# Order of the out-projection's units, and the tiles of two weight sums, in a short-convolution layer

## The chip, the cores and the metric

One core of a Trainium2 chip runs the whole program. The metric is the device time of one execution in microseconds (us): the median of three runs, 1556.54 us before the change (1554.22 to 1557.58).

## What is computed

With these sizes `DEPTH` is 1, so only layer 0 and the final norm run:

```
x: 1024 tokens x 2048
h = rmsnorm(x, norm0_w)
b, c, u, z = split(h @ w_in, 4)             # w_in 2048 x 8192
conv = causal depthwise width-3 convolution of (c * u)
y = b * conv * silu(z)
x = x + y @ w_out                           # w_out 2048 x 2048
out = rmsnorm(x, norm_f_w)
```

## The kernel before

Both projections are done with fewer products than the plain scheme needs. Operands are cut in two along each axis, and seven products of sums of the quarters take the place of eight. Every float32 operand is split in a high part (a copy made by ScalarE, line 111) and a low part (a subtraction on VectorE, line 112), and a product takes three passes: high by high, high by low, low by high.

The program is a list of *steps*, here called units. A unit loads weights (and operands), makes sums, splits, issues 24 matmuls of 512 columns and evacuates the sums from PSUM. The loop of lines 796 to 822 walks over the list: at unit i it issues the loads of some units ahead (line 798), the splits up to unit i + 2, the matmuls and the evacuation of unit i, one *chore* (`chore_at`) and up to two pieces of `background` work. The framework then orders each engine's instructions by readiness, and it places the waits. Tiles come from pools: `t4` (16 tiles of 4 KB a partition, for loads, sums and the 2 `wf` tiles), `xp` (14 of 8 KB, of which the 8 row blocks `st` hold one each at the end) and `wp` (3 of 8 KB, split weights). A tile is given again when its last reader is done, a storing DMA included.

*The chores.* During the in-projection's first half the chores form sums of `w_out` and store them in DRAM: `out_weights` loads the four quarters `wp` (line 706), forms four sums (lines 714 to 719) and stores each (`td`, line 711, issued by GpSimd). All of it runs on VectorE between the splits of the in-projection. The tile named `b[0, 0]` takes the first, the third and the fourth sum, one over the other.

*The out-projection.* It has 32 units of a first kind (`out_step`: four u for each of eight pairs r, db) and then 21 of a second kind (`out_second`: product p of z). Units of the first kind compute four of the seven products of the outer cut: r, in halves db, accumulated over u in four PSUM banks. They load 1 MB (two transfers, pieces of 4 and 2 KB) and split two tiles. The units of the second kind do the other three outer products z, each again by seven (p). They load 1.5 MB (three transfers, pieces of 1 and 2 KB), split three tiles, and end each with two adds of a bank to `st`. A group of the first kind ends at u = 3 with 4 or 8 adds to `st` (line 545). When a block of `st` is complete it is squared for the norm (line 548) and multiplied by the norm's weight (`weigh`, line 555). The last block of a row block calls `finish` (line 739): the scale by the row's norm and two output stores, one from SP's queue and one from ScalarE's. SP's queue also issues all loads, in order.

*Order.* Before, all 32 units of the first kind run ahead of the 21 of the second, and the groups of the first kind take turns on banks `po` 0 to 3 and 4 to 7 (line 579). Units of the second kind use pairs of banks by a table (line 647).

Of the kernel before, what the change touches and what calls it, by code (L numbers as in the profile page):

```python
# [10 lines left out]
AF = mybir.ActivationFunctionType  # L11
ALU = mybir.AluOpType
# [5 lines left out]
NB = 512  # L18
# [23 lines left out]
def hybrid_kernel(  # L42
# [48 lines left out]
    def f4(name, dtype=F32):  # L91
        return t4.tile([P, 1024], dtype, name=name, tag="t4")
# [445 lines left out]
    yv = y_dram.rearrange("(u j h) p t -> h p u j t", j=2, h=2)  # L538
    sv = s_dram.rearrange("u j p s t -> u p j s t")

    def result(th, tb, chunk, ps, final, now, last, scratch):

        cols = slice(chunk * NB, (chunk + 1) * NB)
        v = st[th, tb][:, cols]
        add(v, ps, v)
        if not final:
            return
        nc.scalar.activation(scratch if scratch is not None else ps, v, AF.Square, accum_out=sums[th, tb][:, chunk:chunk + 1])
        if last:
            finish(th, tb, chunk)  # L550
            return

        def weigh():
            c = chunk % 2 * NB
            nc.vector.tensor_tensor(v, v, wf[chunk // 2][:, c:c + NB], op=ALU.mult)

        if now:
            weigh()
        else:
            scaled.append(weigh)  # L560

    def out_step(r, db, u):

        w = {}

        def loads():
            w["b"] = f4(f"wo_{db}_{r}_{u}")
            nc.sync.dma_start(w["b"], w_out[db, 0, 0, u] if r == 1 else t_dram[r][db, u])
            w["y"] = f4(f"ys_{db}_{r}_{u}")
            src = yv[0, :, u, :, ycols[0]] if r == 1 else sv[u, :, :, S_SLOT[r]]  # L570
            nc.sync.dma_start(w["y"].rearrange("p (j t) -> p j t", j=2), src)

        def split_w():
            w["w"] = hl(wp, f"wo_{db}_{r}_{u}")
            split(w["b"], w["w"][:, 0, :], w["w"][:, 1, :])
            w["yh"] = hl(xp, f"Y_{db}_{r}_{u}")
            split(w["y"], w["yh"][:, 0, :], w["yh"][:, 1, :])

        first = 4 * (db if r != 5 else 1 - db)

        def mm():
            open_banks()
            for jj in range(2):
                for tb in range(4):
                    for yz, wz in PASSES:
                        nc.tensor.matmul(  # L586
                            po[first + tb],
                            w["yh"][:, yz, jj * NB + tb * P:jj * NB + (tb + 1) * P],
                            w["w"][:, wz, jj * NB:(jj + 1) * NB],
                            start=(r in (1, 5) and u == 0 and jj == 0 and yz == 0 and wz == 0),  # L590
                            stop=(r in (7, 5) and u == 3 and jj == 1 and yz == 1),
                            skip_group_check=True,
                        )

        def evac():
            if u < 3:
                return
            dest = {1: [(0, 0)], 5: [(0, 1), (1, 1)], 6: [(0, 1)], 7: [(1, 0), (1, 1)]}[r]
            sq = f4(f"sq_{db}")[:, 0:NB] if r == 7 else None
            for tb in range(4):  # L600
                for th, dh in dest:
                    result(th, tb, 2 * dh + db, po[first + tb], r == 7 and dh == 1, False, False, sq)

        return Step(loads, nothing, split_w, mm, evac)

    def out_second(z, p):
# [37 lines left out]
                split(w["b"][v], t[:, 0, :], t[:, 1, :])  # L644
                w["w"].append(t)

        pair = {2: (0, 1, 2), 3: (3, 2, 1), 4: (0, 1, 2)}[z]["acb".index({5: "c", 3: "c", 2: "b"}.get(p, "a"))]
        end = z == 4 and p == 4

        def mm():  # L650
# [10 lines left out]
                    )  # L661

        def evac():
            t2, db, final = {
                1: (0, 0, False), 5: (1, 1, False), 6: (0, 1, False), 2: (0, 0, True),
                7: (1, 1, True), 3: (0, 1, True), 4: (1, 0, True),
            }[p]
            sq = f4(f"sqz_{z}")[:, 0:NB] if p == 7 else None
# [29 lines left out]
    def out_weights(db, u):  # L698
# [9 lines left out]
        def diff(r, o, x0, x1):  # L708
# [86 lines left out]

    for i, s in enumerate(steps):
        early = i < 2
        upto("load", i + (2 if i < 4 else 3 if i < 8 else LOAD_AHEAD + 1 if i < first_out - 8 else 5))
        while late:
            reload_x(late.pop(0))  # L800
        if i == 8 + 7 * 15 - 1:
            reload_x(PRODUCTS[-1])
        n = i - first_out
        for db in range(2):
            m = n - 9 * db
            if m in (-1, 0, 4, 5):
                for tb in range(2):
                    open_rows(int(m > 0), tb + 2 * (m in (0, 5)), db)
# [52 lines left out]
```

## Time and profile before

| | |
|---|---|
| three timed runs | 1554.22, 1556.54, 1557.58 us |
| the profiled execution's own time | 1551.41 us |
| its span, first to last instruction | 1549.6 us |
| granted TensorE clock, mean | 0.995 of full speed |
| PE busy, VectorE busy, ScalarE busy | 98%, 74%, 35% |
| out-projection's matmuls in the trace | 1246.14 to 1536.85 us |

TensorE is busy nearly all the time, so its busy share says little. What can be read is how many matmuls start in a stretch: at full pace 111 or 112 in 25 us, since 24 matmuls take 5.44 us. A stretch with fewer has a wait in it or a lower granted clock. In the rows, `PEld` is TensorE's weight load and `SPq`, `POOLq`, `ACTq` are DMA issues of these engines' queues. A helper records splits (line 112), sums (115) and adds (118), so tiles tell which work a row is.

### The profile page before, as it was taken

The numbers are of one execution on the slowest core, as the hardware profiler recorded it, in microseconds if no ns is written. First come the engines' busy times: TensorE is split into PE (matmuls) and PEld (weight loads), VectorE is DVE, ScalarE is ACT, GpSimd is POOL, SyncE is SP. The second block draws the span as 40 slices with busy tenths as digits, with TensorE's granted clock in tenths as the row PEclk, the third lists the DMA queues.
The fourth block names the chain that finished last, engine by engine and source line by source line (L and its number), as shares of the span: only waits on it lengthen the run. The fifth ranks groups of instructions, "written<-read, shape, count | busy, mean of one in ns | idle before, by whom it ended". The sixth has DMA issues, their size and how long they took to land.

```text
span 1549.6 us, 17709 instructions
## 1 busy us (share of the span) xinstructions
PE 1525.7 (98%) x6705; PEld 1259.1 (81%) x6705; DVE 1141.2 (74%) x1321; ACT 542.0 (35%) x660; POOL 128.2 (8%) x234
## 2 busy tenths in 40 slices
PE   9999999999899999999999999999999999999996
PEld 7878888888688888888888888888888888888884
DVE  6798676776666565457878788887888786568996
ACT  5544343332233333322222222222222334344674
POOL 0001111111111110110000000000000120000000
PEclk9999999999999999999999999999999999999998
DMA  9606677998877665794436444643454679665875
GB/s 364 247 28 212 240 266 271 368 352 329 289 279 257 218 232 176 282 410 150 134 129 201 152 128 138 202 151 114 161 179 163 247 255 396 221 208 189 278 238 228
DMA packets 114277, 351.95 MB, mean 227 GB/s; under 512 B 11008, under 2 KB 22288, under 8 KB 112400
## 3 DMA queue, kind: packets, MB, share of 16 engines
q1 hardware_dynamic: 81040, 223.38, 43.0%
q0 software_dynamic: 31712, 122.72, 20.5%
q10 hardware_dynamic: 1440, 4.73, 0.8%
q8 instruction: 52, 0.85, 0.2%
q14 instruction: 33, 0.27, 0.1%
HBM read 243.83 MB, written 106.96 MB: 226 GB/s over the span
## 4 chain that ended last, share of the span: by engine, by line
PE 71%; issue 14%; DMA 5%; DVE 5%; POOL 3%; ACT 0%; SPq 0%; POOLq 0%; DVEq 0%; ACTq 0%
PE pa L481 32%; PE pc L481 16%; PE po L586 11%; PE pb L481 8%; PE po L654 4%; DMA xsq<-in_x_dram 2%; DMA xr<-in_x_t_dram 1%; POOL td L711 1%; POOL xd L179 1%; POOL pd L513 1%; DMA out_dram<-st 1%; DVE X L112 1%; DMA wz<-w 1%; DVE xc L348 0%; DVE wzh L112 0%
## 5 line engine op out<-in xcount | busy, mean ns | idle before, releaser
L481 PE MATMUL pa<-X,w 128*128 128x512 f32 x2880 | 670.3, 390 | 6.8 <-DVE g L118 5.7
L481 PEld LDWEIGHTS pa<-X,w 128*128 128x128 f32 x2880 | 542.0, 188 | 120.5 <-issue 6.1
L481 PE MATMUL pc<-X,w 128*128 128x512 f32 x1440 | 336.4, 389 | 0.0
L481 PEld LDWEIGHTS pc<-X,w 128*128 128x128 f32 x1440 | 270.3, 188 | 56.1
L112 DVE TENSOR_TENSOR w<-wi,w 128x1024 fp32r<-128x1024 f32 x150 | 183.1, 1222 | 116.1 <-ACT w L111 115.3
L111 ACT CAST w<-wi 128x1024 fp32r<-128x1024 f32 x150 | 157.0, 1049 | 230.8 <-PE pa L481 131.3
L586 PE MATMUL po<-wo,Y 128*128 128x512 f32 x768 | 174.2, 389 | 0.0
L586 PEld LDWEIGHTS po<-wo,Y 128*128 128x128 f32 x768 | 144.2, 188 | 29.9
L481 PE MATMUL pb<-X,w 128*128 128x512 f32 x720 | 168.3, 389 | 0.0
L481 PEld LDWEIGHTS pb<-X,w 128*128 128x128 f32 x720 | 135.1, 188 | 28.4 <-DVE w L112 0.4
L111 ACT CAST w<-wt 128x1024 fp32r<-128x1024 f32 x60 | 63.3, 1055 | 242.1 <-PE pb L481 108.2
L118 DVE TENSOR_TENSOR g<-pa,g 128x512 f32<-128x512 f32 x150 | 102.5, 686 | 28.3 <-PE pa L481 27.3
L654 PE MATMUL po<-wzh,Yz 128*128 128x512 f32 x504 | 114.7, 389 | 2.1 <-DVE st L118 2.1
L654 PEld LDWEIGHTS po<-wzh,Yz 128*128 128x128 f32 x504 | 94.5, 188 | 22.1 <-issue 2.5
L507 ACT COPY g<-pa 128x512 f32<-128x512 f32 x90 | 53.0, 588 | 139.0 <-PE pa L481 138.7
L115 DVE TENSOR_TENSOR wt<-wi,wi 128x1024 f32<-128x1024 f32 x60 | 73.4, 1223 | 34.3 <-DMA s_dram<-g 15.2
L368 PE MATMUL pc<-xc,wc 128*128 128x512 f32 x384 | 87.5, 390 | 1.1 <-DVE wc L353 1.1
L368 PEld LDWEIGHTS pc<-xc,wc 128*128 128x128 f32 x384 | 71.9, 188 | 17.2 <-issue 2.0
L112 DVE TENSOR_TENSOR w<-wt,w 128x1024 fp32r<-128x1024 f32 x60 | 73.2, 1220 | 10.0 <-ACT w L111 10.0
L118 DVE TENSOR_TENSOR g<-pc,g 128x512 f32<-128x512 f32 x90 | 61.5, 686 | 22.4 <-PE pc L481 22.4
L115 DVE TENSOR_TENSOR wp<-wp,wp 128x1024 f32<-128x1024 f32 x32 | 38.9, 1221 | 46.0 <-issue 28.2
L112 DVE TENSOR_TENSOR wo<-wo,wo 128x1024 fp32r<-128x1024 f32 x32 | 39.1, 1222 | 35.8 <-ACT wo L111 35.8
(110 smaller groups left out, 1058.3 us busy)
## 6 DMA issues: line engine op xcount, KB each, us to landing
wi<-in_w_in_dram SPq DMA_DIRECT2D x120, 512.0 KB, 5.0
pd<-g POOLq DMA_DIRECT2D x60, 512.0 KB, 5.6
g<-pd SPq DMA_DIRECT2D x60, 512.0 KB, 4.7
wp<-in_w_out_dram SPq DMA_DIRECT2D x32, 512.0 KB, 6.7
td<-wp POOLq DMA_DIRECT2D x32, 512.0 KB, 5.7
xd<-xo POOLq DMA_DIRECT2D x28, 512.0 KB, 5.9
X<-xd POOLq DMA_DIRECT2D x14, 1024.0 KB, 10.8
w<-wq POOLq DMA_DIRECT2D x24, 512.0 KB, 4.0
```

The lines of the kernel that those rows point to most:

```text
L111: nc.scalar.copy(h, raw)
L112: nc.vector.tensor_tensor(l, raw, h.bitcast(F32), op=ALU.subtract)
L115: nc.vector.tensor_tensor(o, a, b, op=ALU.subtract)
L118: nc.vector.tensor_tensor(o, a, b, op=ALU.add)
L179: nc.gpsimd.dma_start(x_dram[r][:, j], o)
L368: nc.tensor.matmul(state["ps"][2 * s + gi][h], wv[:, wz, gi, jj, s, :], xs[:, xz, h * NB:(h + 1) * NB], start=(a == 0 and jj == 0 and wz = ...
L481: nc.tensor.matmul(ps[where, s], wv[:, wz, j, s, :], xt[:, j % 2, xz, :], start=(r in (1, 5, 2) and j == 0 and wz == 0 and xz == 0), stop= ...
L507: nc.scalar.copy(o, ps[where, s])
L513: nc.gpsimd.dma_start(p_dram[c][i], g[i])
L586: nc.tensor.matmul(po[first + tb], w["yh"][:, yz, jj * NB + tb * P:jj * NB + (tb + 1) * P], w["w"][:, wz, jj * NB:(jj + 1) * NB], start=(r ...
L654: nc.tensor.matmul(po[2 * pair + tb], w["yh"][:, yz, u * 256 + tb * P:u * 256 + (tb + 1) * P], w["w"][u // 2][:, wz, (u % 2) * NB:(u % 2 + ...
L711: nc.gpsimd.dma_start(t_dram[r][db, u], b[o])
```

## The change

1. The list `OUT_PRODUCTS` has another order, and a new list `SECOND` gives the order z = 2, 3, 4 and p = 1, 5, 6, 3, 7, 2, 4 (before: p = 1, 5, 6, 2, 7, 3, 4).
2. From the 9th unit of the first kind on, each is followed by a unit of the second kind, but for those numbered in `NO_SECOND_AFTER`; the last two units of the second kind (z = 4, p = 2 and 4) stand at the end.
3. Units of the first kind all use banks 0 to 3, but for r = 5, db = 0 (banks 4 to 7); those of the second kind use pairs 2 and 3, that is banks 4, 5 and 6, 7, in turn.
4. `result` counts the adds that a block of `st` still has to get (`expect`, `to_come`). Where a block is complete, its square is written to the small tile `idle`, in place of a `t4` tile or the PSUM bank. A block's weighing goes to the background list, and the last block of a row block first does the weighings that are still to do.
5. Loads run one unit further ahead in the out-projection, and the second half of each `st` block is loaded two units earlier.
6. In `out_weights` the third sum is written over the quarter `b[1, 1]` and the fourth over `b[1, 0]`, which are quarters that no store reads.

```diff
-OUT_PRODUCTS = ((1, 0), (5, 0), (6, 0), (1, 1), (7, 0), (6, 1), (5, 1), (7, 1))
+OUT_PRODUCTS = ((1, 0), (5, 0), (6, 0), (7, 0), (5, 1), (1, 1), (6, 1), (7, 1))
+SECOND = ((2, 3, 4), (1, 5, 6, 3, 7, 2, 4))
+NO_SECOND_AFTER = (0, 1, 9, 13, 17)
...
+    def result(th, tb, chunk, ps):
...
         add(v, ps, v)
-        if not final:
+        to_come[th, tb, chunk] -= 1
+        if to_come[th, tb, chunk]:
             return
-        nc.scalar.activation(scratch if scratch is not None else ps, v, AF.Square, accum_out=sums[th, tb][:, chunk:chunk + 1])
-        if last:
+        nc.scalar.activation(idle, v, AF.Square, accum_out=sums[th, tb][:, chunk:chunk + 1])
+        weighs = pending.setdefault((th, tb), [])
+        if len(weighs) == 3:
+            for f in weighs:
+                f()
             finish(th, tb, chunk)
             return
...
-        first = 4 * (db if r != 5 else 1 - db)
+        first = 4 * ((r, db) == (5, 0))
...
-        pair = {2: (0, 1, 2), 3: (3, 2, 1), 4: (0, 1, 2)}[z]["acb".index({5: "c", 3: "c", 2: "b"}.get(p, "a"))]
+        pair = 3 if p in (5, 3, 2) else 2
...
-            diff(6, (0, 0), (1, 1), (0, 0)),
-            diff(4, (0, 0), (1, 0), (0, 0)),
+            diff(6, (1, 1), (1, 1), (0, 0)),
+            diff(4, (1, 0), (1, 0), (1, 1)),
...
-    for r, db in OUT_PRODUCTS:
-        for u in range(4):
-            steps.append(out_step(r, db, u))
-    for z in (2, 3, 4):
-        for p in PRODUCTS:
-            steps.append(out_second(z, p))
+    one = [out_step(r, db, u) for r, db in OUT_PRODUCTS for u in range(4)]
+    two = [out_second(z, p) for z in SECOND[0] for p in SECOND[1]]
+    for i, step in enumerate(one):
+        steps.append(step)
+        if i >= 8 and i - 8 not in NO_SECOND_AFTER:
+            steps.append(two.pop(0))
+    steps.extend(two)
...
-        upto("load", i + (2 if i < 4 else 3 if i < 8 else LOAD_AHEAD + 1 if i < first_out - 8 else 5))
+        upto("load", i + (2 if i < 4 else 3 if i < 8 else LOAD_AHEAD + 1 if i < first_out - 8 else 5 if i < first_out else 6))
...
-            m = n - 9 * db
+            m = n - 7 * db
```

How this moves instructions is shown at three places. The first is VectorE in the in-projection, from the second weight sum of one set (`wp_1_2`) to the add that empties a bank of block 8 (`pa_0_8_0`). Before:

```order
L115 TENSOR_TENSOR wp_1_2_01_2794<-wp_1_2_11_2798,wp_1_2_01_2794 128x1024
L115 TENSOR_TENSOR wp_1_2_00_2792<-wp_1_2_11_2798,wp_1_2_00_2792 128x1024
L112 TENSOR_TENSOR w_0_8_3_2876<-wi_0_8_11_2607,w_0_8_3_2876 128x1024
L118 TENSOR_TENSOR g_8_0_2786<-pb_0_8_0_2879,g_8_0_2786 128x512
L115 TENSOR_TENSOR wp_1_2_00_2792<-wp_1_2_10_2796,wp_1_2_00_2792 128x1024
L115 TENSOR_TENSOR wp_1_3_00_2907<-wp_1_3_01_2909,wp_1_3_00_2907 128x1024
L118 TENSOR_TENSOR g_8_2_2788<-pb_0_8_1_2892,g_8_2_2788 128x512
L112 TENSOR_TENSOR w_0_8_4_2917<-wt_0_8_2684,w_0_8_4_2917 128x1024
L115 TENSOR_TENSOR wt_0_9_2950<-wi_0_9_01_2838,wi_0_9_00_2800 128x1024
L118 TENSOR_TENSOR g_8_1_2787<-pa_0_8_0_2760,g_8_1_2787 128x512
```

With the change:

```order
L117 TENSOR_TENSOR wp_1_2_01_2794<-wp_1_2_11_2798,wp_1_2_01_2794 128x1024
L117 TENSOR_TENSOR wp_1_2_11_2798<-wp_1_2_11_2798,wp_1_2_00_2792 128x1024
L117 TENSOR_TENSOR wp_1_2_10_2796<-wp_1_2_10_2796,wp_1_2_11_2798 128x1024
L114 TENSOR_TENSOR w_0_8_3_2876<-wi_0_8_11_2607,w_0_8_3_2876 128x1024
L120 TENSOR_TENSOR g_8_0_2786<-pb_0_8_0_2879,g_8_0_2786 128x512
L117 TENSOR_TENSOR wp_1_3_00_2907<-wp_1_3_01_2909,wp_1_3_00_2907 128x1024
L120 TENSOR_TENSOR g_8_2_2788<-pb_0_8_1_2892,g_8_2_2788 128x512
L114 TENSOR_TENSOR w_0_8_4_2917<-wt_0_8_2684,w_0_8_4_2917 128x1024
L117 TENSOR_TENSOR wt_0_9_2950<-wi_0_9_01_2838,wi_0_9_00_2800 128x1024
L120 TENSOR_TENSOR g_8_1_2787<-pa_0_8_0_2760,g_8_1_2787 128x512
```

The fourth sum (into `wp_1_2_10`, before into `wp_1_2_00`) moves ahead by two rows and stands right behind the third; the rest keeps its order.

The second place is the third unit of the group r = 6, db = 0, in SP's queue (loads: `wo` and `ys` of a unit of the first kind, `yz` and two `wz` of one of the second) and on VectorE. SP before, and with the change:

```order
L568 DMA wo_0_6_2_8743<-td_6_165 128x1024
L571 DMA ys_0_6_2_8745<-s_dram_174 128x2x512
L568 DMA wo_0_6_3_8777<-td_6_165 128x1024
L571 DMA ys_0_6_3_8779<-s_dram_174 128x2x512
L568 DMA wo_1_1_0_8819<-in_w_out_dram 128x1024
L571 DMA ys_1_1_0_8821<-y_dram_92 128x2x512
```

```order
L580 DMA wo_0_6_2_8707<-td_6_165 128x1024
L583 DMA ys_0_6_2_8709<-s_dram_174 128x2x512
L637 DMA yz_2_1_8747<-y_dram_92 128x4x256
L648 DMA wz_2_1_0_8749<-in_w_out_dram 128x2x512
L648 DMA wz_2_1_1_8751<-in_w_out_dram 128x2x512
L580 DMA wo_0_6_3_8785<-td_6_165 128x1024
```

VectorE before, from a split of unit u = 3 over the eight adds of the group r = 5 to the split of u = 2's weights:

```order
L112 TENSOR_TENSOR Y_0_6_3_8864<-ys_0_6_3_8779,Y_0_6_3_8864 128x1024
L118 TENSOR_TENSOR st_0_0_8436<-po_4_8529,st_0_0_8436 128x512
L118 TENSOR_TENSOR st_1_0_8667<-po_4_8529,st_1_0_8667 128x512
L118 TENSOR_TENSOR st_0_1_8439<-po_5_8530,st_0_1_8439 128x512
L118 TENSOR_TENSOR st_1_1_8670<-po_5_8530,st_1_1_8670 128x512
L118 TENSOR_TENSOR st_0_2_8513<-po_6_8531,st_0_2_8513 128x512
L118 TENSOR_TENSOR st_1_2_8707<-po_6_8531,st_1_2_8707 128x512
L118 TENSOR_TENSOR st_0_3_8516<-po_7_8532,st_0_3_8516 128x512
L118 TENSOR_TENSOR st_1_3_8710<-po_7_8532,st_1_3_8710 128x512
L112 TENSOR_TENSOR wo_0_6_2_8825<-wo_0_6_2_8743,wo_0_6_2_8825 128x1024
```

And with the change:

```order
L114 TENSOR_TENSOR wzh_2_1_1_8875<-wz_2_1_1_8751,wzh_2_1_1_8875 128x1024
L120 TENSOR_TENSOR st_0_0_8436<-po_4_8533,st_0_0_8436 128x512
L120 TENSOR_TENSOR st_1_0_8671<-po_4_8533,st_1_0_8671 128x512
L120 TENSOR_TENSOR st_0_1_8439<-po_5_8534,st_0_1_8439 128x512
L120 TENSOR_TENSOR st_1_1_8674<-po_5_8534,st_1_1_8674 128x512
L120 TENSOR_TENSOR st_0_2_8517<-po_6_8535,st_0_2_8517 128x512
L120 TENSOR_TENSOR st_1_2_8711<-po_6_8535,st_1_2_8711 128x512
L120 TENSOR_TENSOR st_0_3_8520<-po_7_8536,st_0_3_8520 128x512
L120 TENSOR_TENSOR st_1_3_8714<-po_7_8536,st_1_3_8714 128x512
L114 TENSOR_TENSOR wo_0_6_2_8835<-wo_0_6_2_8707,wo_0_6_2_8835 128x1024
```

In front of the eight adds, and so in front of the split of `wo_0_6_2`, stands now the split of `wzh_2_1_1`, whose load is the third behind `ys_0_6_2`; before it was that of `Y_0_6_3`, whose load is the second.

The third place is VectorE in the last units, from the last split to the first row sum of `finish` (`TENSOR_REDUCE tot_1_0`). Before:

```order
L112 TENSOR_TENSOR wzh_4_4_1_10527<-wz_4_4_1_10445,wzh_4_4_1_10527 128x1024
L118 TENSOR_TENSOR st_1_2_8707<-po_0_8525,st_1_2_8707 128x512
L118 TENSOR_TENSOR st_1_3_8710<-po_1_8526,st_1_3_8710 128x512
L118 TENSOR_TENSOR st_1_0_8667<-po_2_8527,st_1_0_8667 128x512
L555 TENSOR_TENSOR st_1_2_8707<-st_1_2_8707,wf_0_9003 128x512
L555 TENSOR_TENSOR st_1_3_8710<-st_1_3_8710,wf_0_9003 128x512
L742 TENSOR_REDUCE tot_1_0_10587<-sums_1_0_8668 128x1
L118 TENSOR_TENSOR st_1_1_8670<-po_3_8528,st_1_1_8670 128x512
L743 TENSOR_SCALAR tot_1_0_10587<-tot_1_0_10587 128x1
L118 TENSOR_TENSOR st_1_2_8707<-po_0_8525,st_1_2_8707 128x512
L749 SCALAR_TENSOR_TENSOR st_1_0_8667<-st_1_0_8667,r_1_0_10590,wf_0_9003 128x512
```

With the change, from the last of the group's eight adds:

```order
L120 TENSOR_TENSOR st_1_3_8714<-po_3_8532,st_1_3_8714 128x512 x2
L114 TENSOR_TENSOR wzh_4_4_0_10514<-wz_4_4_0_10395,wzh_4_4_0_10514 128x1024
L569 TENSOR_TENSOR st_1_0_8671<-st_1_0_8671,wf_0_9025 128x512
L120 TENSOR_TENSOR st_1_2_8711<-po_4_8533,st_1_2_8711 128x512
L120 TENSOR_TENSOR st_1_3_8714<-po_5_8534,st_1_3_8714 128x512
L569 TENSOR_TENSOR st_1_0_8671<-st_1_0_8671,wf_1_9027 128x512
L569 TENSOR_TENSOR st_1_1_8674<-st_1_1_8674,wf_0_9025 128x512
L569 TENSOR_TENSOR st_1_1_8674<-st_1_1_8674,wf_1_9027 128x512
L569 TENSOR_TENSOR st_1_2_8711<-st_1_2_8711,wf_1_9027 128x512
L569 TENSOR_TENSOR st_1_2_8711<-st_1_2_8711,wf_0_9025 128x512
L569 TENSOR_TENSOR st_1_3_8714<-st_1_3_8714,wf_1_9027 128x512
L569 TENSOR_TENSOR st_1_3_8714<-st_1_3_8714,wf_0_9025 128x512
```

Two more adds and then the row sum of block 0 follow. So from the end of the last unit of the first kind to the first row sum VectorE now has twelve adds, a split and eight weighings; before, three adds and two weighings stood behind the last split.

## Rows read from the trace of the kernel before

**Rows 1.** The page's first part: engine, busy time (share of the span), instructions.

```profile
PE 1525.7 (98%) x6705; PEld 1259.1 (81%) x6705; DVE 1141.2 (74%) x1321; ACT 542.0 (35%) x660; POOL 128.2 (8%) x234
```

**Rows 2.** Stretches of 25 us: busy time (instructions), PEclk, DMA share, GB/s.

```profile
350.00:375.00 25.00, 25.00 (x112) 20.71 (x111) 14.53 (x15) 8.38 (x11) 4.25 (x8) 1.00 0.81 299
375.00:400.00 25.00, 19.55 (x86) 15.57 (x84) 14.45 (x14) 4.62 (x6) 3.20 (x6) 0.95 0.88 307
400.00:425.00 25.00, 24.75 (x100) 20.36 (x101) 17.07 (x19) 8.29 (x13) 4.78 (x9) 0.91 0.85 309
425.00:450.00 25.00, 25.00 (x112) 20.68 (x112) 19.17 (x23) 6.75 (x8) 4.26 (x8) 1.00 0.88 314
```

**Rows 3.** Waits from 265 to 420 us: us in total, times, longest.

```profile
DVE wp L115 <- issue: 28.2, 5, 6.7
...
DVE wp L115 <- DMA td<-wp: 13.4, 6, 4.0
...
PE pa L481 <- DVE g L118: 5.7, 1, 5.7
```

**Rows 4.** The timeline about 390 us: start, us, engine, line, operation, count, [idle, releaser].

```profile
378.36 8.93 SPq L706 DMA_DIRECT2D wp<-in_w_out_dram  x4
...
385.70 1.23 DVE L115 TENSOR_TENSOR wp<-wp,wp 128x1024 f32<-128x1024 f32 x1 [3.96 <-DMA td<-wp]
...
387.22 0.53 POOL L711 DMA_DIRECT2D td<-wp  x1 [4.66 <-DVE wp L115]
...
388.94 5.60 PE L481 MATMUL pc<-X,w 128*128 128x512 f32 x24
...
394.28 2.36 DVE L115 TENSOR_TENSOR wp<-wp,wp 128x1024 f32<-128x1024 f32 x2 [5.61 <-issue]
...
400.25 13.14 PE L481 MATMUL pa<-X,w 128*128 128x512 f32 x48 [5.71 <-DVE g L118]
...
413.23 5.63 PE L481 MATMUL pc<-X,w 128*128 128x512 f32 x24
```

**Rows 5.** The chain that ended last, out-projection: start, us, engine, line, count.

```profile
1246.14 174.08 PE po L586 x768
1420.22 62.42 PE po L654 x276
```

**Rows 6.** The timeline about 1290 us, ScalarE and VectorE.

```profile
1285.89 1.05 ACT L111 CAST Y<-ys 128x1024 fp32r<-128x1024 f32 x1 [4.53 <-DMA ys<-s_dram]
...
1291.90 1.05 ACT L111 CAST Y<-ys 128x1024 fp32r<-128x1024 f32 x1 [4.01 <-DMA ys<-s_dram]
...
1294.12 4.87 DVE L118 TENSOR_TENSOR st<-po,st 128x512 f32<-128x512 f32 x8
...
1295.39 1.05 ACT L111 CAST Y<-ys 128x1024 fp32r<-128x1024 f32 x1 [2.44 <-DMA ys<-y_dram]
...
1298.91 1.22 DVE L112 TENSOR_TENSOR wo<-wo,wo 128x1024 fp32r<-128x1024 f32 x1
```

**Rows 7.** The hardware queue, 1290 to 1320 us: packets, MB, share of 16 engines.

```profile
q1 hardware_dynamic: 4258, 10.84, 94.1%
```

**Rows 8.** The same queue from 1420 to 1490 us.

```profile
q1 hardware_dynamic: 13012, 19.02, 83.1%
```

**Rows 9.** The timeline of the last 50 us.

```profile
1505.18 1.41 SPq L756 DMA_DIRECT2D out_dram<-st  x2
...
1518.48 1.05 ACT L111 CAST Yz<-yz 128x1024 fp32r<-128x1024 f32 x1 [4.61 <-DMA yz<-zd]
...
1531.13 5.72 PE L654 MATMUL po<-wzh,Yz 128*128 128x512 f32 x24 [2.12 <-DVE st L118]
```

**Rows 10.** The same timeline, rows of VectorE that weigh and scale.

```profile
1532.10 1.28 DVE L555 TENSOR_TENSOR st<-st,wf 128x512 f32<-128x512 f32 x2
...
1534.78 0.74 DVE L749 SCALAR_TENSOR_TENSOR st<-st,r,wf 128x512 f32<-128x512 f32 x1
...
1542.72 0.75 DVE L749 SCALAR_TENSOR_TENSOR st<-st,r,wf 128x512 f32<-128x512 f32 x1 [0.66 <-POOL r L745]
```

More of the change, by code (lines that the diff above doesn't have):

```diff
@@ L539, in hybrid_kernel, with expect @@
     sv = s_dram.rearrange("u j p s t -> u p j s t")
-    def result(th, tb, chunk, ps, final, now, last, scratch):
+    to_come, pending = {}, {}
+    def expect(blocks):
+        for b in blocks:
+            to_come[b] = to_come.get(b, 0) + 1
+    def result(th, tb, chunk, ps):
         cols = slice(chunk * NB, (chunk + 1) * NB)
@@ L545, in result @@
         add(v, ps, v)
-        if not final:
+        to_come[th, tb, chunk] -= 1
+        if to_come[th, tb, chunk]:
             return
-        nc.scalar.activation(scratch if scratch is not None else ps, v, AF.Square, accum_out=sums[th, tb][:, chunk:chunk + 1])
-        if last:
+        nc.scalar.activation(idle, v, AF.Square, accum_out=sums[th, tb][:, chunk:chunk + 1])
[3 more added lines that the diff above has]
+                f()
             finish(th, tb, chunk)
             return
+        todo = [chunk]
         def weigh():
[L554 to L560, printed above, removed]
+            if todo:
+                c = todo.pop() % 2 * NB
+                nc.vector.tensor_tensor(v, v, wf[chunk // 2][:, c:c + NB], op=ALU.mult)
+        weighs.append(weigh)
+        scaled.append(weigh)
     def out_step(r, db, u):
@@ L577, in split_w @@
             split(w["y"], w["yh"][:, 0, :], w["yh"][:, 1, :])
-        first = 4 * (db if r != 5 else 1 - db)
+        first = 4 * ((r, db) == (5, 0))
+        dest = {1: [(0, 0)], 5: [(0, 1), (1, 1)], 6: [(0, 1)], 7: [(1, 0), (1, 1)]}[r]
+        if u == 3:
+            expect((th, tb, 2 * dh + db) for tb in range(4) for th, dh in dest)
         def mm():
@@ L597, in evac @@
                 return
-            dest = {1: [(0, 0)], 5: [(0, 1), (1, 1)], 6: [(0, 1)], 7: [(1, 0), (1, 1)]}[r]
-            sq = f4(f"sq_{db}")[:, 0:NB] if r == 7 else None
             for tb in range(4):
                 for th, dh in dest:
-                    result(th, tb, 2 * dh + db, po[first + tb], r == 7 and dh == 1, False, False, sq)
+                    result(th, tb, 2 * dh + db, po[first + tb])
         return Step(loads, nothing, split_w, mm, evac)
@@ L645, in split_w @@
                 w["w"].append(t)
-        pair = {2: (0, 1, 2), 3: (3, 2, 1), 4: (0, 1, 2)}[z]["acb".index({5: "c", 3: "c", 2: "b"}.get(p, "a"))]
+        pair = 3 if p in (5, 3, 2) else 2
+        t2, db2 = {1: (0, 0), 5: (1, 1), 6: (0, 1), 2: (0, 0), 7: (1, 1), 3: (0, 1), 4: (1, 0)}[p]
+        dest = [(th, 2 * t2 + tb, 2 * dh + db2) for tb in range(2)]
+        expect(dest)
         end = z == 4 and p == 4
@@ L663, in evac @@
         def evac():
[L664 to L668, printed above, removed]
             for tb in range(2):
-                result(th, 2 * t2 + tb, 2 * dh + db, po[2 * pair + tb], final, True, z > 2 and p in (3, 4), sq)
+                result(*dest[tb], po[2 * pair + tb])
         return Step(loads, nothing, split_w, mm, evac)
```

## The prediction

> **What bounds the kernel now.** I read the page's engine shares, then stretches of 25 us, then waits and timeline where a stretch had too few matmuls. TensorE is busy 98% of the span [rows 1], so a gain can only be time in which it waits or runs at a lower clock. Stretches at full pace hold 112 matmuls; 375 to 400 us holds 86 and 400 to 425 us holds 100, at a granted clock of 0.95 and 0.91 (a mean over both levels, 1.2 and 2.4 GHz) [rows 2]. That is the one large hole before the last 20 us.
>
> The timeline shows what it is. A unit's matmuls start at 388.94 us, and a unit takes 5.44 us (174.08 us for 32) [rows 5]. So the next should start at 394.38; it starts at 400.25, with 5.71 us of waiting for a VectorE add to `g`, which has to empty the bank. The two units from there take 13.14 us where 10.88 is the pace; the third starts at 413.23 in place of 405.26 [rows 4]. The loss is 413.23 - 405.26 = 7.97 us: 5.87 late, 2.10 at the lower clock. VectorE was late because of the chores: the third weight sum waited 3.96 us for a store of `wp` (385.70), the fourth another 5.61 us (394.28); the store of the third sum had been issued at 387.22 [rows 4]. The page calls the second releaser "issue", it sees none; but the fourth sum writes the tile that this store reads, and it starts 7.06 us after the issue. From 265 to 420 us such waits sum to 28.2 + 13.4 = 41.6 us in eleven pieces [rows 3]. TensorE felt them once.
>
> In the out-projection TensorE keeps its pace to the last unit: 53 units from 1246.14 would end at 1534.46, the last ends at 1531.13 + 5.72 = 1536.85 [rows 5, 9]. So 2.39 us are lost there. Behind it lies a tail of 1549.60 - 1536.85 = 12.75 us.
>
> **The change, part by part.**
>
> *Weight sums 3 and 4.* They now overwrite quarters that no store reads, so the eleven waits have no cause. The number of sums, stores and loads is the same. VectorE then would have the third sum done 3.96 us earlier, and the rows from the fourth sum to the add that frees the bank are a split, two adds of 512 columns and two sums. Four rows at 1.22 us or about it [rows 4, 6] and two adds at 0.61 (4.87 us for eight [rows 6]) are some 6 us; from the add at 388 us on, they end before TensorE needs the bank at 394.38. So I take the whole 7.97 us. The other bound is nothing: the sums also need the next set's quarters, whose four loads SP issued only from 378.36 to 387.3 [rows 4], since its queue waits for tiles too, and two tiles of a set are now held until their stores land. Value: -8.0 us, bounds -8 and 0.
>
> *Alternating units.* The same 53 units run, at the same pace, so only waits count. The wait before the last unit (2.39 us) comes from loads: the output stores of four row blocks (4 MB) stood ahead of loads in SP's queue, up to 1505.18, and a load of the last but one unit kept ScalarE waiting 4.61 us, to 1518.48 [rows 9]. Now these four row blocks are complete after unit 42, eleven units before the end, and VectorE has the splits of two kinds mixed instead of three a unit at the end. I take -2.4 us, bounds -2.4 and +2 (the loads behind the stores are then only those of the last three units, but they are still behind them).
>
> *The alternation starts in a full DMA queue.* From 1290 to 1320 us the hardware queue alone takes 94.1% of the engines [rows 7]. There ScalarE gets its operand tiles late (waits of 4.53, 4.01, 2.44 us) and the split of `wo_0_6_2` on VectorE, behind the eight adds, ends at 1298.91 + 1.22 = 1300.13; its unit, the 11th, starts at 1246.14 + 10 x 5.44 = 1300.54. The margin is 0.41 us [rows 5, 6]. With the change the split in front of the eight adds waits for the third load behind `ys_0_6_2`, not the second. Loads land at 1285.89, the second behind it at 1291.90, the fourth at 1295.39 [rows 6], so the third at about 1293.65, 1.75 later. The new loads have pieces of 1 and 2 KB: at a full queue the old mix moves 10.84 MB / 30 us / 0.941 = 384 GB/s, the small pieces 19.02 / 70 / 0.831 = 327 [rows 7, 8], so 15% slower, 0.4 us more. 1.75 + 0.4 - 0.41 gives a wait of 1.8 us. Bounds: 0, where the store traffic clears first, and 4.1, at three loads of 3.0 us (the pace to 1291.90) times 384 / 327. Waits of 2 us cost no clock: after the one of 2.12 us a unit took 5.72 [rows 9]. Behind this unit the splits gain on TensorE again, since a unit of either kind needs less DMA time (1.5 MB / 327 = 4.6 us) than its 5.44.
>
> The Trainium skill, "Perfetto Trace Analysis", DMA Optimizations, says that DMAs below 2 KB have significant overhead and that larger pieces fill the memory's bandwidth better; it speaks against moving the small-piece loads into this stretch. If it meant half the rate rather than the 15% that the rows show, this term would be some 7 us.
>
> *The tail.* From the end of the last unit of the first kind VectorE has, before the first `finish`, twelve adds at 0.61, a split at 1.22 and eight weighings at 0.65 (1.28 for two [rows 10]): 7.3 + 1.2 + 5.2 = 13.7 us; then a row sum, the power on GpSimd and the first scale, about 1.2 us: 14.9. TensorE ends 3 x 5.44 = 16.3 after that point. So the first scale starts 1.4 us before its end; before, it was 1536.85 - 1534.78 = 2.07 [rows 10]. The four scales follow as before (1534.78 to 1542.72), so the tail grows by 0.7; ScalarE's squares now stand behind its scales for two blocks, about 0.6 each, of which I count one: +1.2 us, bounds -1 and +3.
>
> *At no cost:* squares into `idle` (same instruction, ScalarE has slack), the loads of `st` two units earlier and loads one unit further ahead (they were limited by free tiles, not by the loop). If that cover is gone, it shows as part of the 1.8 us.
>
> Sum: -8.0 - 2.4 + 1.8 + 1.2 = -7.4 us. The profiled execution took 1551.41 us, 1.8 more than its span; so 1544.0. The timed runs before lie 2.8 to 6.2 us above it, their median 5.1. Whether this excess stays is unknown. The hole at 394 us hangs on when stores land and is what can differ most between executions, so part of the excess should go with it. With all of it gone the time is 1544.0, with none 1549.1; I take 1547, between them.
>
> **Rivals.**
>
> *A: the front wait changes its name.* SP's queue still gets tiles only as stores land, so the sums wait for loads in place of stores. For: the four loads spread over 8.9 us [rows 4]. Against: before, the fourth sum's partner behind it ran without a wait. At half the hole, 4 us come back: 1551 to 1553, 1552.
>
> *B: the small-piece loads keep the queue full.* The alternation then is late not by one unit but by several: at 3.0 us a transfer of 512 KB (the pace while `st` is loaded, [rows 6]) a unit of the second kind needs 9 us, 3.6 more than TensorE. Against: the `st` traffic ends; for: the margin is 0.41 us already. Two such units cost 7 us, so 1554; from four on the kernel is slower than before.
>
> *C: banks.* Every group but one now ends and begins on banks 0 to 3. If VectorE does the adds of a group only when the unit between has gone by, TensorE waits for them: twice eight adds and three times four, 28 x 0.61 = 17 us, so 1547 + 17 = 1564, slower. It decides from the point where VectorE starts a group's adds over 4 us late (a bank's two adds take 1.2, the unit between 5.44). Against: VectorE is busy 74% [rows 1], and mixing evens it out; for: splits of two units stand ahead of the adds. The Trainium skill, "Perfetto Trace Analysis", Optimizing Tensor Performance, says that independent groups should rotate through banks, so that evacuation overlaps the next group; by that rule alone the change goes the wrong way, and the 17 us are its price. Here the unit between rotates, on banks 4 to 7.
>
> **How the numbers follow.** Forecast 0.64, A 0.14, B 0.14, C 0.08. About 0.2%, 3.1 us, can be told from no change: below 1553.4 is faster, above 1559.7 slower. The forecast's own range is 1541 (excess and the 11th unit's wait gone) to 1551. A gives half to faster, half to the same; B 0.06 faster, 0.06 same, 0.02 slower; C all slower. So faster 0.77, same 0.13, slower 0.10. The range 1541 to 1554 holds the forecast, A, and B up to two units.
>
> **What would show it.** Right: no stretch of 25 us around 375 to 425 below 110 matmuls, and no VectorE wait for stores of `wp`; a TensorE wait of 1 to 3 us at the 11th unit of the out-projection; none before the last unit; a tail near 14 us. Wrong: a wait at 394 us under another name (A), waits at several units from the 12th on (B), or TensorE waiting for adds to `st` at group ends (C). The forecast falls if the timed median stays above 1553.

## The result, and the profile after

The changed kernel takes 1540.42 us (median of four runs, 1539.93 to 1541.50); the kernel before took 1557.05 beside it. The ratio is 0.9898, interval 0.9881 to 0.9915: 1% faster, 16.6 us. The forecast was 1547, 9.5 us below the 1556.54 known then; the median lies 0.6 us below the range's lower end of 1541. The profiled execution took 1541.50 us (1539.7 span), 9.9 less than that of before. In a later series the same kernel took 1541.62 (before 1555.92), so a difference of 1 us between series tells nothing.

The engines, as in [rows 1]:

```profile
PE 1523.5 (99%) x6705; PEld 1257.5 (82%) x6705; DVE 1143.7 (74%) x1321; ACT 542.0 (35%) x660; POOL 128.2 (8%) x234
```

The stretches that held the hole (columns of [rows 2]):

```profile
375.00:400.00 25.00, 25.00 (x112) 20.67 (x112) 19.92 (x21) 6.84 (x9) 5.06 (x10) 1.00 1.00 373
400.00:425.00 25.00, 25.00 (x112) 20.71 (x111) 15.24 (x18) 8.96 (x12) 1.83 (x4) 1.00 0.74 288
```

Both hold 112 matmuls at a granted clock of 1.00; before it was 86 and 100 at 0.95 and 0.91. Then all waits of TensorE (what it waited for: us in total, times, longest):

```profile
PE warm L101 <- DVE pw L207: 1.2, 1, 1.2
PE pa L483 <- ACT w L113: 1.1, 1, 1.1
PE po L601 <- DVE wo L114: 0.9, 1, 0.9
PE pc L370 <- DVE wc L355: 0.9, 1, 0.9
PE pc L483 <- ACT w L113: 0.7, 1, 0.7
```

No wait is longer than 1.2 us, and only the third, for the split of `wo`, lies in the out-projection. On VectorE the same view, its two longest rows, for 265 to 420 us:

```profile
DVE w L114 <- ACT w L113: 36.0, 13, 4.2
DVE wp L117 <- DMA wp<-in_w_out_dram: 11.2, 3, 4.3
```

The 41.6 us of waiting for stores in eleven pieces [rows 3] are gone; 11.2 us in three pieces are for loads of the sums' quarters (before, 4.1 in two). VectorE is idle nearly as long as before: 36.0 us of it now wait for ScalarE's copies (before, 4.5). What changed is which work stands behind the idle time, and TensorE feels none of it. In the timeline the first of the two adds that empty the banks `pa` is done at 390.75 + 0.68 = 391.43 us, 4.0 us before the unit that writes this bank again; before, that unit stood 5.71 us [rows 4]:

```profile
390.75 0.68 DVE L120 TENSOR_TENSOR g<-pa,g 128x512 f32<-128x512 f32 x1
...
395.46 4.92 PE L483 MATMUL pa<-X,w 128*128 128x512 f32 x21
```

The out-projection, by the row of its first ten units, that of the 11th, and that of the last three (start, us, engine, line, operation, [idle, releaser]; the 241st matmul is the first of the 11th unit and needs no low part):

```profile
1238.66 54.79 PE L601 MATMUL po<-wo,Y 128*128 128x512 f32 x241
1294.39 5.51 PE L601 MATMUL po<-wo,Y 128*128 128x512 f32 x23 [0.95 <-DVE wo L114]
```

```profile
1511.90 16.48 PE L670 MATMUL po<-wzh,Yz 128*128 128x512 f32 x72
```

And the tail, the rows that answer to [rows 10]:

```profile
1510.06 4.87 DVE L120 TENSOR_TENSOR st<-po,st 128x512 f32<-128x512 f32 x8 [0.44 <-PE po L601]
...
1524.89 0.75 DVE L760 SCALAR_TENSOR_TENSOR st<-st,r,wf 128x512 f32<-128x512 f32 x1 [0.65 <-POOL r L756]
...
1533.00 0.75 DVE L760 SCALAR_TENSOR_TENSOR st<-st,r,wf 128x512 f32<-128x512 f32 x1 [0.66 <-POOL r L756]
...
1534.18 0.37 ACTq L768 DMA_DIRECT2D out_dram<-st  x1
```

TensorE ends at 1511.90 + 16.48 = 1528.38 us; the last unit starts without a wait (before 2.12, [rows 9]). The tail is 1539.7 - 1528.38 = 11.3 us (before 12.75).

| piece of the profiled execution | forecast | measured |
|---|---|---|
| start of the out-projection, 1246.14 to 1238.82 us ([rows 5], and the same chain after) | -8.0 | -7.3 |
| late at the 11th unit, 1294.39 - (1238.82 + 54.40) | +1.8 | +1.2 |
| wait before the last unit | -2.4 | -2.4 |
| tail, 12.75 to 11.32 | +1.2 | -1.4 |
| sum | -7.4 | -9.9 |
| timed median above the profiled execution | +3.0 | -1.1 |

Before, the last line was +5.1 us. The first line is the hole's 8.0 us and 0.6 us by which two stretches of before ran slower (units at 377.82 and 821.26 us), less 1.3 us that this execution lost more up to 107 us, where TensorE waits for ScalarE's copies (1.1 and 0.7 in its waits above; 1.0 in all before, 0.8 in the profile of the later series).

### The profile page after: what moved, and what is told of

It reads as the page before. It is cut to its first block, busy times and chain, and to the rows that moved or that the text cites. A ratio compares the mean times of both kernels' runs of the same rounds, so it can differ in the third digit from the quotient of the medians.

```text
span 1539.7 us, 17753 instructions
## 1 busy us (share of the span) xinstructions
PE 1523.5 (99%) x6705; PEld 1257.5 (82%) x6705; DVE 1143.7 (74%) x1321; ACT 542.0 (35%) x660; POOL 128.2 (8%) x234
## 4 chain that ended last, share of the span: by engine, by line
PE 90%; DMA 5%; DVE 4%; issue 1%; ACT 1%; SPq 0%; POOL 0%; POOLq 0%; DVEq 0%; ACTq 0%
PE pa L483 42%; PE pc L483 21%; PE pb L483 11%; PE po L601 9%; PE po L670 7%; DMA xsq<-in_x_dram 2%; DMA wz<-in_w_out_dram 1%; DMA xr<-in_x_t_dram 1%; DVE X L114 1%; DVE xr L148 0%; DVE st L120 0%; DVE xc L350 0%; DVE g L397 0%; DMA wi_c<-in_w_in_dram 0%; DVE st L569 0%
## 5 line engine op out<-in xcount | busy, mean ns | idle before, releaser
L601 PE MATMUL po<-wo,Y 128*128 128x512 f32 x768 | 177.5, 389 | 0.9 <-DVE wo L114 0.9
L114 DVE TENSOR_TENSOR wzh<-wz,wzh 128x1024 fp32r<-128x1024 f32 x42 | 50.9, 1219 | 21.2 <-ACT wzh L113 21.1
L120 DVE TENSOR_TENSOR st<-po,st 128x512 f32<-128x512 f32 x90 | 57.5, 682 | 2.6 <-PE po L670 1.9
```

Of the source, the lines that this page charges most:

```text
L114: nc.vector.tensor_tensor(l, raw, h.bitcast(F32), op=ALU.subtract)
L120: nc.vector.tensor_tensor(o, a, b, op=ALU.add)
L601: nc.tensor.matmul(po[first + tb], w["yh"][:, yz, jj * NB + tb * P:jj * NB + (tb + 1) * P], w["w"][:, wz, jj * NB:(jj + 1) * NB], start=(r ...
```

## The experiments

Times are medians, each beside runs of the kernel before in the same series.

**Only the two weight sums** (`e1`): the kernel before with

```diff
-            diff(6, (0, 0), (1, 1), (0, 0)),
-            diff(4, (0, 0), (1, 0), (0, 0)),
+            diff(6, (1, 1), (1, 1), (0, 0)),
+            diff(4, (1, 0), (1, 0), (1, 1)),
```

> The kernel before with nothing but the new tiles for the third and fourth weight sum. Theory (the terms add up, and the part of the timed median that lies above the profiled execution sits in the front hole): the hole about 394 us is closed, the out-projection starts about 7.5 us earlier than 1246.14, the span is about 1542 and the timed median 1543 to 1546, that is 11 to 13 us less than before. Rival 1 (each term is the same in every execution): the median falls by the 8 us of the profile alone, to 1548 to 1549, and stays some 5 us above the profiled execution. Rival 2 (the front wait changes its name, A of the prediction): a wait of 3 to 6 us for an add to g or for a weight split is left near 394 us, median 1551 to 1553.

Measured: 1542.54 us (1542.01 to 1543.27), before 1556.10 (1551.58 to 1561.31, 15 runs); ratio 0.9905, interval 0.9891 to 0.9919. So 13.6 us, where the profile of before showed a hole of 8, and the spread falls from 9.7 us (standard deviation 2.6, 15 runs) to 1.3 (0.6, four runs). The theory holds, with a gain 0.6 us above its range. The profiled execution has one wait left in the out-projection, the one before the last unit:

```profile
PE po L654 <- DVE st L118: 1.0, 1, 1.0
```

**Only the order** (`e2`): the changed kernel with the two lines of `e1` put back.

> The changed kernel with the old tiles for the third and fourth weight sum, so the new order of the out-projection alone. Theory: the hole of 8 us about 394 us is back, the out-projection and the tail keep what they gained in the profile (1.2 and 1.4 us), so the span is about 1547 and the timed median 1553 to 1555, 2 to 3 us under before. Rival 1 (the excess of the timed runs over the profiled one came from the out-projection's loads and stores): it is gone here too, median 1548 to 1549. Rival 2 (the order gains nothing by itself): within 1 us of before.

Measured: 1553.55 us, ratio 0.9979 (0.9966 to 0.9992), so 2.5 us, as the theory has it, but with a span of 1551.9, not 1547. The two parts sum to 13.6 + 2.5 = 16.1 us; the whole change gave 16.6 in its first series and 14.3 in that of `c1` below. The reason for the longer span is what matters:

```profile
363.13 8.45 PE L483 MATMUL pa<-X,w 128*128 128x512 f32 x36 [2.27 <-DVE g L120]
...
405.41 13.13 PE L483 MATMUL pa<-X,w 128*128 128x512 f32 x48 [5.23 <-DVE g L120]
```

```profile
400.00:425.00 25.00, 19.77 (x79) 16.08 (x79) 21.00 (x23) 6.87 (x10) 5.83 (x11) 0.86 0.81 269
```

In this execution VectorE's waits for stores of `wp` (48.1 us) hold TensorE in four places instead of one (two are shown; 0.38 and 1.10 us the others), the granted clock of 400 to 425 us falls to 0.86, and the out-projection starts at 1250.86, 12.0 us later than in `e1` (1238.81). The hole is not one size: it is 8.0 us in one execution and 12.0 in another. This is what spread the runs of before, and put their median above the profiled one: with the sums' waits gone both are gone, with nothing else changed (`e1`); with the waits back and the new order kept (`e2`), the eleven runs spread over 5.0 us again.

**Only the fourth sum** (`e3`): the kernel before with `diff(4, (1, 0), (1, 0), (0, 0))`.

> The kernel before, with the fourth weight sum in its own quarter (b[1, 0], formed as b[1, 0] - b[0, 0]) and the third still over the first sum's tile, as before. Theory: the third sum still waits up to 4 us for the store of the first, the fourth no longer waits 5.6; VectorE's add that empties the bank comes 5.6 us earlier than 400.25, so at 394.6, when TensorE wants it at 394.4: a wait of at most 0.5 us is left, no lower clock, and the median is within 1 us of the run with both sums moved. Rival 1 (either wait alone is enough, because VectorE has no slack there): TensorE still waits 2 us or more, the median lies half way, 1549 to 1551. Rival 2 (A): as with both, a wait under another name.

Measured: 1542.70 us, ratio 0.9905 (0.9891 to 0.9919), the same as `e1`. VectorE's waits for the sums' tiles from 265 to 420 us:

```profile
DVE wp L115 <- DMA td<-wp: 11.7, 7, 3.8
DVE wp L115 <- DMA wp<-in_w_out_dram: 7.8, 3, 3.8
```

The third sum still waits for stores, 3.8 us at the longest, and TensorE does not notice. So the theory holds: taking away the fourth sum's waits, which the page calls "issue", is enough to close the hole; moving the third was not needed. Moving the third alone was not run.

**The changed kernel once more** (`c1`).

> The changed kernel itself once more, as the run beside which the next three are read. Every theory: 1539.5 to 1541.5, with runs within 1 us of each other, since the hole that made the runs before differ is gone.

Measured: 1541.62 us (1540.19 to 1541.96), 0.1 above what was expected, with runs 1.8 us apart instead of 1. In its profile the wait at the 11th unit is 1.71 us where the first profile had 0.95.

**The alternation one unit later** (`e4`) **and one earlier** (`e8`): `NO_SECOND_AFTER` (0, 1, 2, 9, 13, 17) and (0, 9, 13, 17, 21).

> The changed kernel with the alternation starting one unit later (no unit of the second kind behind the third unit of the group r = 6, db = 0 either; so three of them stand at the end). Theory: in front of the split of wo_0_6_2 stands again a split whose load is the second behind it, so the wait of 0.95 us at the 11th unit of the out-projection goes; 1539 to 1539.8. Rival 1 (the full queue is what is late, wherever the alternation starts): a wait of about 1 us at the 12th to 14th unit, 1540.4. Rival 2 (three units of the second kind at the end bring back a wait for loads there): the last units wait 1 to 2 us, 1541 to 1542.

> The changed kernel with the alternation starting one unit earlier (a unit of the second kind behind the second unit of the group r = 6, db = 0, none behind the second unit of r = 1, db = 1). Theory (loads through a full queue set when the first unit of the second kind can start, and each of them adds 0.5 MB, 1.3 us at 380 GB/s): the wait near 1290 us grows from 1.0 to 2 to 3 us, 1541.5 to 1542.5. Rival 1 (only the place of one split behind the eight adds matters): the wait is under 1 us, 1539.5 to 1540.5. Rival 2 (banks: the second kind's unit stands too near the group on banks 4 to 7): a wait for adds to st, 4 us or more, 1544.

Measured: 1541.63 and 1540.82 us. The wait, a row of TensorE for each:

```profile
1293.43 10.99 PE L601 MATMUL po<-wo,Y 128*128 128x512 f32 x47 [1.89 <-DVE wo L114]
```

```profile
1293.48 5.51 PE L670 MATMUL po<-wzh,Yz 128*128 128x512 f32 x23 [1.21 <-DVE wzh L114]
```

Both theories fall. Started later, the wait does not go; started earlier, it does not grow beyond 1.2. But `e4` is no test of its theory's reason: the split in front of the eight adds is there not one whose load is the second behind `ys_0_6_2`, as it says, but that of `Yz_2_1`, whose load is the third, and it stands there beside that of `Y_0_6_3`: one split more than in the kernel before. In all three kernels a unit starts late at 1293 to 1295 us, and no later unit waits: rival B has no price wherever the alternation starts.

**The loads as before** (`e5`): 5 units ahead in place of 6, and `m = n - 9 * db`.

> The changed kernel with the two parts that I costed at nothing undone: loads one unit less ahead in the out-projection, and the second half of each st block loaded two units later. Theory: nothing but the wait at the 11th unit changes, by half a microsecond at most either way, 1540 to 1541. Rival 1 (they are needed, because the units of the second kind add to these halves from the 14th unit on): TensorE or VectorE waits for st there, 2 to 5 us, 1542.5 to 1545.5. Rival 2 (the earlier st loads are what fills the queue at the 11th unit): its wait of 0.95 us goes, 1539.3.

Measured: 1541.68 us beside 1541.62 of `c1`; wait at the 11th unit 1.24. That is above the expected 1540 to 1541, but so is `c1`: the two edits cost and bring nothing that can be measured, as costed.

**Which split stands ahead of the adds** (`e9`, `e10`): in `e9` the other weight split of the unit (2, 1), in `e10` none.

```diff
-                t = hl((wp, xp)[v], f"wzh_{z}_{p}_{v}")
+                t = hl((wp, xp)[v if (z, p) != (2, 1) else 1 - v], f"wzh_{z}_{p}_{v}")   # e9
+                t = hl(wp if v == 0 or (z, p) == (2, 1) else xp, f"wzh_{z}_{p}_{v}")      # e10
```

> The changed kernel with the two split weights of the unit (2, 1) in each other's pools, so that the split that stands in front of the eight adds, and so of wo_0_6_2, is that of wzh_2_1_0, whose load is issued one transfer earlier than that of wzh_2_1_1. Theory (that split's load sets the 11th unit's wait): the eight adds start 0.8 to 1.5 us earlier than at 1288.34, the wait of 1.0 to 1.7 us falls to 0.5 us or less, 1539.5 to 1540.8. Rival 1 (the whole queue is late there, another split takes its place): the wait stays above 0.9 us, 1541.6 as in the last run of the changed kernel.

> The changed kernel with both split weights of the unit (2, 1) in the pool wp (three tiles), so that none of its weight splits stands in front of the eight adds. Theory: the adds start right behind the split of wo_0_6_1, at 1287 or earlier, and the 11th unit waits 0.3 us or less; but the 12th, whose two weight splits now stand behind a load more, may wait up to 1.5 us, so 1540 to 1541.5. Rival 1 (the queue is late for both): the waits of both sum to what the 11th had, 1541.6. Rival 2 (the pool with three tiles runs dry): a wait of 3 us or more at the 12th or 13th unit, 1544.

Measured: 1540.64 and 1539.10 us (1538.41 to 1541.49). VectorE of the changed kernel, of `e9` and of `e10` at the place:

```profile
1284.48 1.23 DVE L114 TENSOR_TENSOR Yz<-yz,Yz 128x1024 fp32r<-128x1024 f32 x1 [4.20 <-ACT Yz L113]
...
1287.20 1.22 DVE L114 TENSOR_TENSOR wzh<-wz,wzh 128x1024 fp32r<-128x1024 f32 x1 [0.36 <-ACT wzh L113]
1288.34 4.87 DVE L120 TENSOR_TENSOR st<-po,st 128x512 f32<-128x512 f32 x8
1293.13 1.21 DVE L114 TENSOR_TENSOR wo<-wo,wo 128x1024 fp32r<-128x1024 f32 x1
```

```profile
1283.96 1.23 DVE L114 TENSOR_TENSOR Yz<-yz,Yz 128x1024 fp32r<-128x1024 f32 x1 [4.62 <-ACT Yz L113]
...
1286.23 1.22 DVE L114 TENSOR_TENSOR wzh<-wz,wzh 128x1024 fp32r<-128x1024 f32 x1
1287.37 4.87 DVE L120 TENSOR_TENSOR st<-po,st 128x512 f32<-128x512 f32 x8
```

```profile
1285.58 1.23 DVE L114 TENSOR_TENSOR Yz<-yz,Yz 128x1024 fp32r<-128x1024 f32 x1 [4.23 <-ACT Yz L113]
1286.72 1.22 DVE L114 TENSOR_TENSOR wo<-wo,wo 128x1024 fp32r<-128x1024 f32 x1
1287.86 4.87 DVE L120 TENSOR_TENSOR st<-po,st 128x512 f32<-128x512 f32 x8
```

And TensorE of `e10`:

```profile
1239.65 60.00 PE L601 MATMUL po<-wo,Y 128*128 128x512 f32 x264
```

From the first matmul of the out-projection to the adds it is 49.7 us in the changed kernel (1288.34 - 1238.66), 49.7 in `e9` (first matmul 1237.63), 48.2 in `e10`. There the first 11 units (264 matmuls) run through in one row: no wait, and none behind. The executions differ in when the split of `Yz` starts, which waited over 4 us for its load. Measured from its start, the adds begin 3.86 us later in the changed kernel (3.84 in `c1` and `e5`), 3.41 in `e9`, 2.28 in `e10` (2.27 in `e12` below, which has the same pools). So the later load is worth 0.45 us, and the split itself, 1.2 us of work, 1.1 more. The theory of `e9` falls, since 0.45 us does not take the wait away (1.01 in `e9`). That of `e10` holds in its mechanism, with a time 0.9 us below its range. The median of `e10` lies 1.5 us below that of `e9`, but the runs of the two overlap; its profiled execution began the out-projection 1 us late, so its span (1539.6) does not show the gain. In `e4` too a split more than before stands there: its adds begin 50.6 us behind the first matmul (1287.38 - 1236.76), those of the kernel before 48.2 (1294.12 - 1245.97).

**No unit between groups on the same banks** (`e11`): `NO_SECOND_AFTER` (0, 1, 3, 7, 11).

> The changed kernel with other places left out of the alternation: at the ends of the groups (r = 6, db = 0), (7, 0) and (5, 1) no unit of the second kind stands between a group and the next on the same banks 0 to 3. Rival C of the prediction, at its full price: TensorE waits for 4, 8 and 8 adds of 0.61 us, 12 us, 1553. Theory (a group's banks end one after the other, so VectorE can start 2 us before the group's end and the next group comes back to each bank 2 us after its last matmul; only two adds a bank are 0.54 us slower than three matmuls): 0, 0.8 and 0.8 us, and up to 4 us more where VectorE is in the middle of splits; waits for adds to st of 1.6 to 6 us, 1543 to 1547. Rival 2 (nothing is felt): 1541.

Measured: 1541.55 us. All of TensorE's waits:

```profile
PE pc L370 <- DVE wc L355: 1.4, 1, 1.4
PE po L601 <- DVE wo L114: 1.2, 1, 1.2
PE warm L101 <- DVE pw L207: 1.2, 1, 1.2
PE pa L483 <- ACT w L113: 1.1, 1, 1.1
```

None is for an add to `st`; the one for `wo` is the 11th unit's. My price of 1.6 to 6 us falls too: nothing is felt, as in rival 2. Rival C was priced as if all adds of a group began when the group ends. Here a group's banks end one after the other, and VectorE begins with them. At the end of the group (7, 0) the next group follows at once on the same banks, two units in one row:

```profile
1342.72 11.08 PE L601 MATMUL po<-wo,Y 128*128 128x512 f32 x48
```

```profile
1346.32 4.88 DVE L120 TENSOR_TENSOR st<-po,st 128x512 f32<-128x512 f32 x8
```

The group ends at 1342.72 + 5.44 = 1348.16 us; its eight adds start 1.8 us before, and the two units take 11.08 us where two others take 11.04.

**The tail** (`e7`, `e12`). In `e7` each `finish` of the last blocks is held back by one block (`late_finish(1)` runs the one held before), so that the next square can go first:

```diff
-            finish(th, tb, chunk)
+            late_finish(1)
+            held.append(lambda: finish(th, tb, chunk))
```

In `e12`, on top of `e10`, two row blocks are complete with the last unit but two:

```diff
-... for z in SECOND[0] for p in SECOND[1]]
+... for z in SECOND[0] for p in (SECOND[1] if z != 4 else (1, 5, 6, 3, 2, 7, 4))]
-        end = z == 4 and p == 4
+        end = z == 4 and p in (7, 4)
```

> The changed kernel with finish of each of the last four row blocks issued one block later, so that the sum of squares of the next block stands ahead of ScalarE's scaling of this one. Theory (ScalarE sets the pace of the tail: in the profile of the changed kernel the last square waits from 1529.17, when its add is done, to 1531.26, behind a scaling of 1.15 us): the tail shrinks from 11.3 to 9.8 us, 1538.9. Rival 1 (the tail hangs on the power on GpSimd and the output stores): 1540.4, no change. Rival 2 (the scalings that are now late delay ScalarE's own output stores): 1541.

> The changed kernel with two edits: the pools of the run e10 (adds first), and for z = 4 the order p = 1, 5, 6, 3, 2, 7, 4 in place of 1, 5, 6, 3, 7, 2, 4, with the unit p = 7 doing its two banks one after the other, as p = 4 does. Row blocks 0 and 1 of the second half are then complete with the last unit but two, and only blocks 2 and 3 with the last. Theory (before and after alike, 13.6 us pass from the first output store of the last four row blocks to the end, in which 4.2 MB leave at about 400 GB/s; so the tail hangs on how early the first of them is scaled): blocks 0 and 1 are scaled some 5 us earlier, their 2.1 MB have left by TensorE's end, and the tail is the add, square, power and scale of block 3 (3.8 us) and its store (3.5 to 5 us): 7.5 to 9 us in place of 11.3; with the 11th unit's wait gone, 1535.5 to 1537.5. Rival 1 (the tail is a chain of VectorE and ScalarE through the four blocks, not of stores): the eight weighings now stand between the scales, the tail stays at 10.5 to 11.5 us, 1539 to 1540. Rival 2 (two units running on banks 4 and 5 make TensorE wait for adds to st): 1 to 3 us lost before the last unit, 1538 to 1540.

Measured: `e7` 1540.54 us (beside 1541.62 of `c1`), `e12` 1539.57 (1538.26 to 1540.02). TensorE ends at 1511.29 + 16.48 = 1527.77 and 1510.32 + 16.48 = 1526.80 us, so the tails are 10.9 us (to 1538.7) and 11.0 (to 1537.8), 0.3 to 0.4 less. In `e7` the last square still ran behind a scaling, so its theory (9.8) was not put to the test and the time is that of its rival 1. `e12`, scales and last store:

```profile
1518.93 0.75 DVE L760 SCALAR_TENSOR_TENSOR st<-st,r,wf 128x512 f32<-128x512 f32 x1 [0.44 <-POOL r L756]
...
1521.84 0.75 DVE L760 SCALAR_TENSOR_TENSOR st<-st,r,wf 128x512 f32<-128x512 f32 x1 [0.44 <-POOL r L756]
...
1527.38 0.75 DVE L760 SCALAR_TENSOR_TENSOR st<-st,r,wf 128x512 f32<-128x512 f32 x1 [0.65 <-POOL r L756]
...
1528.45 0.68 DVE L120 TENSOR_TENSOR st<-po,st 128x512 f32<-128x512 f32 x1
...
1530.92 0.75 DVE L760 SCALAR_TENSOR_TENSOR st<-st,r,wf 128x512 f32<-128x512 f32 x1 [0.66 <-POOL r L756]
...
1532.10 0.37 ACTq L768 DMA_DIRECT2D out_dram<-st  x1
```

Two blocks are scaled 4.9 us or more before TensorE's end, as meant, and the tail is nearly as long as ever: my theory that stores set it falls, and tail and time are those of its rival 1. It is now the chain of the last block alone: its add waits for the scaling of the block ahead (1528.45, 1.65 us behind TensorE), the scale comes 2.47 later, the store is issued 1.18 after that, and from the issue to the end it is 5.7 us, with the queues free. In the changed kernel that is 5.5 (1534.18 to 1539.7); there the four scales still follow one another in 8.1 us.

`e10` and `e12` have the lowest medians, 0.9 to 2.5 us under the two of the changed kernel. In both the profile has no wait at the 11th unit; by their intervals (0.9877 to 0.9911, 0.9879 to 0.9909) they are not told from it.

## Why the prediction was right, and where not

*The direction and the main cause* were right. The hole about 394 us was the sums' waits for stores, and it went with them alone (`e1`).

*Its size was the failed step.* The prediction says: "The hole at 394 us hangs on when stores land and is what can differ most between executions, so part of the excess should go with it": I let 2.1 of 5.1 us go. All went, and the timed runs now lie below the profiled one. The hole is worth 13.6 us in the timed runs (`e1` against before), not the 8.0 of one profiled execution; `e2`'s profile, with 12.0, shows how. So the term for the excess came out 4.1 us lower (-1.1 in place of +3.0), of the 6.6 us by which the forecast missed; the tail is 2.6 more, the rest of the terms nearly cancel. The spread of three timed runs (3.4 us) and the profiled run below all of them were known; they could have told me that the profiled hole might be a small one.

*Rival A* had its mechanism without its price: the wait did change its name, to loads and to ScalarE's copies, and VectorE's add had 4.0 us to spare.

*The 11th unit* was the right place and nearly the right size (1.8 forecast; 1.2, and 1.7 of waiting in `c1`). But the working rested on the third load being later than the second, and the split stood idle only 0.36 us for what hangs on it. `e9` and `e10` give the load 0.45 us and the split itself 1.1. That the size came near is luck.

*Before the last unit* the 2.4 us came as forecast. That they are the old order's is shown by `e1` (1.03 us there) and `e3` (1.91), which keep it; the wait varies.

*The tail* had the wrong sign. I counted 14.9 us from the end of the last unit of the first kind to the first scale; it is 1524.89 - 1512.06 = 12.8. VectorE starts the adds 2.0 us before that end, because the banks are complete one after the other. So the first scale comes 3.5 us before TensorE's end, not 1.4 (before 2.07), and the last 4.6 behind it (before 1542.72 - 1536.85 = 5.9, [rows 10]); the squares behind ScalarE's scales added 0.2 us to the four scales' 7.9, not 0.6 or more.

*Rival B* did not come: at the full queue of 1290 to 1320 us

```profile
q1 hardware_dynamic: 5924, 10.44, 95.9%
```

10.44 MB / 30 us / 0.959 = 363 GB/s are 5.5% under the 384 of [rows 7], though the mean packet fell from 2.5 to 1.8 KB. Beside 1297 to 1327 us of before, the same stretch of the program, it is 4.5% (10.69 MB at 93.8%, 380 GB/s). I had 15%, from a queue that was busy 83%. The rule that I weighed there (the Trainium skill, "Perfetto Trace Analysis", DMA Optimizations: DMAs below 2 KB have significant overhead) has at most this price here, though packets under 2 KB rose from 366 of 4566 to 2397 of 6215; whether it is the small pieces or the rest of the mix is not shown.

*Rival C* has no price, by `e11`. The rule weighed there (the Trainium skill, "Perfetto Trace Analysis", Optimizing Tensor Performance: independent groups should rotate through banks) is met within a group here: its four banks, done one after the other, give VectorE the 2 us.

## What to carry to other kernels

A stall that hangs on when a DMA lands need not have one size: where timed runs spread, and lie above the profiled execution, the stall in the profile may be a small sample; here taking away its cause took most of the spread too. Before a transfer or a wait is blamed for a late engine, swap only that and measure from a fixed event: here the extra split on VectorE cost the adds 1.1 us, the lateness of its load 0.45. Price an evacuation from the end of its own bank, not of the unit: here it began 1.8 to 2.0 us earlier.

## What the runs showed of the hardware

From the issue of the last 512 KB output store to the end of the span it takes 5.5 us in the changed kernel, 5.7 in `e12`, where the queues ahead of it are free, and 5.9 in `e7` (1532.83 to 1538.7), where the stores stand closer. Bringing earlier stores forward gained 0.3 us of the tail at most (`e12`). TensorE's waits of 1.89 us (`e4`, 1275 to 1300 us, 102 matmuls) and 2.27 us (`e2`, 350 to 375 us, 100 matmuls) left the granted clock of their 25 us at 1.00, the level of 2.4 GHz; with the wait of 5.23 us in `e2` the mean of its 25 us fell to 0.86, with that of 5.71 us before to 0.91 [rows 2, 4], a mix with the level of 1.2 GHz.
